# A two-layer, two-block transformer on one core: the scheduler's rule for choosing an engine, and new step orders for its four mixers

## The chip, the cores and the metric

The kernel runs on 1 core of a Trainium2 chip. The metric is the device time of one launch in microseconds (us), the median of several runs. Engines are named as in the profile: PE (matrix products), DVE (vector), ACT (scalar), POOL (GpSimd), SP (issues DMAs).

## What is computed

Sequence 512, width 1024, batch 1, fp32. Two blocks follow each other, each of two layers, and every layer is a mixer and a feed-forward network with residuals and RMS norms:

```python
# first block
h = h + nsa_mixer(rms_norm(h), ...)       # 16 heads: compressed, selected and window attention, gated
h = h + conv_ffn(rms_norm(h), ...)        # d_ff 2816, width-3 convolution, silu gate
h = h + swa_sink_mixer(rms_norm(h), ...)  # sliding window with sinks, its own k and v norm
h = h + conv_ffn(rms_norm(h), ...)
# second block
x = x + even_mixer(rmsnorm(x), ...)       # window attention beside a multi-scale pool
x = x + sq_relu_mlp(rmsnorm(x), ...)      # d_ff 4096, (relu u)^2
x = x + odd_mixer(rmsnorm(x), ...)        # dense attention beside a bidirectional recurrence
x = x + sq_relu_mlp(rmsnorm(x), ...)
return rmsnorm(x)
```

In the traces the stretches are, roughly: nsa to 390 us, conv_ffn to 780, swa to 900, conv_ffn to 1300, even to 1410, mlp to 1830, odd to 1990, mlp to the end.

## The kernel before

Activations lie transposed, as 128 x 512 tiles. Each fp32 operand of a large product is split in a high and a low half in a format that PE takes at full rate, and a product is three matmuls: high x high, high x low, low x high. `load` (L824) brings one unit of weights, 128 x 1024, by a 512 KB DMA into a `raw` buffer (4 of them), makes the high half with `copy` (L777) and the low half `raw - high` with `sub` (L803), both into one of 3 `W` buffers. `proj` (L841) is a load and 24 matmuls of 512 columns.

The program isn't emitted as it is written. A recorder notes every operation, and `Recorder.order` (L507) plays them through a model of five engines: it goes from event to event, and at each a free engine takes the first operation of its ready list that finds its buffers free. What it writes out is a fixed sequence for each engine. An operation may name other engines that could do it (`alt`). Before the change another engine takes one only where the work queued on the home engine reaches a bound for that pair of engines (`SPILL`, L352, tested at L617 to L620). Home engines: `copy` and `affine` ACT with DVE as the other, `tt` with `spare` (and so `sub`) DVE with POOL as the other, `norm` (L796, the softmax division) POOL with DVE, `ptt` (L800) POOL alone, `square` ACT with POOL.

In the mixers the recorded order of the steps (projections `Q`, `K`; scores `a`; products `p`; halves `L`, `U` of the output projection; and so on) is a string in `ORDERS` (L357), which `play` (L1054) walks through.

Functions the prediction speaks of: `norm_out` (L917) is the epilogue of a layer's last product: for each of 8 columns it adds to the residual, splits gain x residual (`split`: a copy and one multiply-subtract), and adds the square into the sum for the norm. `stats` (L1756) turns that sum into a factor per token: transposes, a reduce, a small multiply-add, a power on POOL, transposes, a copy. `tables` (L966) multiplies the two rotary tables by it. `rope` (L973) copies a projection from PSUM, has its halves swapped by DMA, and makes two products and an add. `qstack` (L991) splits the result into two stacked operands of 64 partitions each, two copies and two subtractions, and only then can the scores' matmuls of that query start.

Of the kernel before, what the change touches and what calls it, by code (L numbers as in the profile page):

```python
# [15 lines left out]
P = 128  # L16
# [321 lines left out]
def _width(v):  # L338
# [15 lines left out]
BOOST = 0  # L354
DMAQ = 2.0
HORIZON = 3000
ORDERS = {  # L357
# [33 lines left out]
class Recorder:  # L391
# [115 lines left out]
    def order(self):  # L507
# [31 lines left out]

        def oldest(kind):  # L540
            w = waiting[kind]
            while first[kind] < len(w) and w[first[kind]] in given:
                first[kind] += 1
            return w[first[kind]] if first[kind] < len(w) else -1
# [49 lines left out]
        while left:  # L594
# [7 lines left out]
            for e in engines:  # L602
# [7 lines left out]
                while i < min(len(ready[e]) - 1, 200):  # L610
# [6 lines left out]
                    if op.eng != e:  # L617
                        queue = sum(o.cost for _, _, o in ready[op.eng][:12] if not o.done)
                        if queue + max(0, free_at[op.eng] - now) < SPILL[op.eng, e]:
                            continue  # L620
                    if e == "scalar" and op.table and table not in op.table and now - op.ready < PATIENCE:
                        if now - switched < PATIENCE or any(not o.table or table in o.table for _, _, o in ready[e][i + 1:]):
                            heapq.heappush(events, max(switched, op.ready) + PATIENCE + 1e-6)
                            continue
# [88 lines left out]
def F(ap):  # L713
    return ap.bitcast(F32)


def _body(tc, ctx, d, out):
# [78 lines left out]
    def norm(o, i, a, b):  # L796
        nc.gpsimd.tensor_scalar(o, i, a, b, op0=OP.mult, op1=OP.mult, alt=[
            ["vector", "tensor_scalar", (o, i, a, b), {"op0": OP.mult, "op1": OP.mult}]])

    def ptt(o, a, b, op):  # L800
        nc.gpsimd.tensor_tensor(out=o, in0=a, in1=b, op=op)
# [171 lines left out]
    def rope(ps, cs, half):  # L973
# [11 lines left out]
        tt(o, sw, cs[1], OP.mult)  # L985
# [75 lines left out]
    def nsa(x, epi, prepare, half):  # L1061
# [189 lines left out]
        def scores(g, qb, ty, h0):  # L1251
# [21 lines left out]
            nc.vector.reciprocal(sm[:, 0:nh], sm[:, 0:nh])  # L1273
            for i, (r, t) in enumerate(who):
# [588 lines left out]
```

## Time and profile before

| | us |
|---|---|
| median of 3 runs (2398.35 to 2403.59) | 2403.03 |
| the profiled execution's own time | 2399.78 |
| its span, first to last instruction | 2397.9 |

| engine | busy us | share of the span |
|---|---|---|
| PE | 2280.3 | 95% |
| DVE | 1760.9 | 73% |
| POOL | 1254.6 | 52% |
| ACT | 701.8 | 29% |

PE's granted clock has a mean of 0.976 of full speed. The times of single instructions overlap a little on one engine, since one starts while the last one drains; the busy times here count such overlap once. The profile gives nearly every instruction the line of `emit` (L698), so tiles and shapes tell groups apart: `W<-raw` is the high half of a weight unit, `W<-raw,W` its low half, `S` a 128 x 512 working tile, `D` a double one, `bank` a PSUM bank, `par` per-channel constants, `small` per-token numbers.

### The profile page before, as it was taken

How to read it: one execution, taken by the hardware profiler on the slowest of the kernel's cores; microseconds unless marked ns; L12 is line 12 of the kernel's file. 1: busy time of each engine (PE TensorE's matmuls, PEld its weight loads, DVE VectorE, ACT ScalarE, POOL GpSimd, SP SyncE). 2: the span in 40 equal slices, each digit the busy share in tenths (PEclk: the TensorE clock that was granted, in tenths of full speed). 3: DMA queues.
4: the chain of work that ended last, by engine and by line, in shares of the span. 5: the costliest groups of instructions: out<-in, count | busy, mean ns of one | idle time of the engine just before them, and what ended most of it. 6: DMA issues, size and time to landing. Idle time of an engine off the chain costs nothing.

```text
span 2397.9 us, 28536 instructions
## 1 busy us (share of the span) xinstructions
PE 2280.3 (95%) x10565; PEld 1857.6 (77%) x10565; DVE 1760.9 (73%) x2429; ACT 701.8 (29%) x1353; POOL 1254.6 (52%) x865
## 2 busy tenths in 40 slices
PE   9878999999999799999999799999999789999998
PEld 7766678888888578888888578888887568888888
DVE  7978888949499999949499897345358899643546
ACT  4435653202023463202014342000014584100003
POOL 5755636444447855444437745444466565444445
PEclk9979999999999899999999899999999989999999
DMA  6421102232225212332225213332243201222224
GB/s 208 137 75 49 54 23 88 97 106 97 97 84 185 87 36 85 101 106 97 97 82 182 71 52 99 102 109 97 97 154 115 66 27 62 97 97 97 97 97 132
DMA packets 77243, 230.02 MB, mean 96 GB/s; under 512 B 10288, under 2 KB 12976, under 8 KB 77104
## 3 DMA queue, kind: packets, MB, share of 16 engines
q1 hardware_dynamic: 75584, 226.89, 29.1%
q8 instruction: 83, 1.36, 0.2%
q10 hardware_dynamic: 1520, 1.32, 0.2%
q14 instruction: 56, 0.46, 0.1%
HBM read 206.67 MB, written 8.39 MB: 90 GB/s over the span
## 4 chain that ended last, share of the span: by engine, by line
PE 56%; DVE 6%; ACT 2%; issue 1%; POOL 1%; SPq 0%; DMA 0%; DVEq 0%; ACTq 0%; POOLq 0%
PE bank L698 56%; DVE S L698 4%; DVE small L698 1%; ACT S L698 1%; DVE D L698 1%; POOL S L698 0%; DVE W L698 0%; ACT W L698 0%; ACT L698 0%; POOL W L698 0%; ACT D L698 0%; SPq L698 0%; DVE bank L698 0%; DMA S<-S 0%; DVEq L1850 0%
## 5 line engine op out<-in xcount | busy, mean ns | idle before, releaser
L698 PE MATMUL bank<-S,W 128*128 128x512 f32 (+1 forms) x7972 | 1809.3, 387 | 9.9 <-POOL W L698 5.9
L698 PEld LDWEIGHTS bank<-S,W 128*128 128x128 f32 x7972 | 1472.6, 189 | 313.3 <-DVE S L698 7.8
L698 POOL TENSOR_TENSOR W<-raw,W 128x1024 fp32r<-128x1024 f32 (+2 forms) x288 | 693.3, 2408 | 708.3 <-DVE W L698 541.8
L698 DVE CAST W<-raw 128x1024 fp32r<-128x1024 f32 (+2 forms) x246 | 179.8, 731 | 460.5 <-issue 319.3
L698 POOL TENSOR_TENSOR S<-S,S 128x512 f32<-128x512 f32 (+3 forms) x203 | 327.4, 1618 | 234.7 <-DVE S L698 157.7
L698 ACT ACTIVATE S<-S 128x512 f32<-128x512 f32 (+2 forms) x220 | 137.4, 627 | 969.6 <-DVE S L698 951.9
L698 DVE TENSOR_TENSOR S<-bank,S 128x512 f32<-128x512 f32 (+5 forms) x429 | 264.5, 632 | 14.5 <-ACT S L698 7.0
L698 DVE SCALAR_TENSOR_TENSOR S<-S,par,S 128x511 f32<-128x511 f32 (+3 forms) x236 | 250.2, 1069 | 7.7 <-ACT S L698 2.6
L698 ACT ACTIVATE W<-raw 128x1024 fp32r<-128x1024 f32 (+2 forms) x132 | 133.7, 1015 | 298.2 <-PE bank L698 242.8
L698 DVE TENSOR_TENSOR S<-S,S 128x512 fp32r<-128x512 f32 (+3 forms) x210 | 193.4, 926 | 16.8 <-ACT S L698 4.7
L698 PE MATMUL bank<-S,D 128*128 128x512 f32 (+3 forms) x387 | 138.4, 431 | 26.1 <-DVE S L698 13.5
L698 DVE CAST S<-S 128x512 fp32r<-128x512 f32 (+1 forms) x126 | 120.2, 954 | 48.7 <-ACT S L698 44.0
L698 ACT ACTIVATE S<-bank,small 128x256 f32<-128x256 f32 (+6 forms) x245 | 127.5, 530 | 83.3 <-DVE small L698 74.8
L698 ACT ACTIVATE S<-bank 128x512 fp32r<-128x512 f32 (+5 forms) x179 | 102.8, 588 | 137.9 <-PE bank L698 116.1
L698 PE MATMUL bank<-D,W 128*128 128x512 f32 x536 | 139.8, 397 | 0.6 <-DVE W L698 0.6
L698 DVE TENSOR_TENSOR W<-raw,W 128x1024 fp32r<-128x1024 f32 (+2 forms) x90 | 124.7, 1385 | 13.6 <-ACT W L698 13.0
L698 PE MATMUL bank<-cst,S 128*128 128x128 f32 x710 | 115.5, 283 | 13.6 <-DVE S L698 7.9
L698 DVE TENSOR_REDUCE small<-bank 128x1 f32<-128x512 f32 (+7 forms) x201 | 119.9, 614 | 6.8 <-PE bank L698 5.2
L698 PEld LDWEIGHTS bank<-D,W 128*128 128x128 f32 x536 | 99.1, 188 | 20.4 <-ACT S L698 0.8
L698 PEld LDWEIGHTS bank<-cst,S 128*128 128x128 f32 x710 | 88.0, 145 | 33.8 <-DVE S L698 8.3
L698 DVE TENSOR_SCALAR S<-S,par 128x512 f32<-128x512 f32 (+1 forms) x62 | 112.3, 1812 | 2.1
L698 PEld LDWEIGHTS bank<-S,D 128*128 128x128 f32 x387 | 70.4, 197 | 51.4 <-DVE S L698 24.9
(122 smaller groups left out, 1398.3 us busy)
## 6 DMA issues: line engine op xcount, KB each, us to landing
raw<-in_f_in_dram SPq DMA_DIRECT2D x88, 512.0 KB, 3.2
raw<-in_m_out_dram SPq DMA_DIRECT2D x72, 512.0 KB, 3.2
raw<-in_m_in_dram SPq DMA_DIRECT2D x64, 512.0 KB, 3.3
raw<-in_f_out_dram SPq DMA_DIRECT2D x32, 512.0 KB, 3.2
raw<-in_a_in_dram SPq DMA_DIRECT2D x17, 512.0 KB, 3.5
raw<-in_o_in_dram SPq DMA_DIRECT2D x15, 512.0 KB, 3.4
S<-S SPq DMA_DIRECT2D x116, 64.0 KB, 2.0
raw<-in_f_out_dram SPq DMA_DIRECT2D x16, 384.0 KB, 2.9
```

What stands on the lines that cost most here:

```text
L698: r = getattr(getattr(nc, op.eng), name)(*args, **kw)
```

## The change

Three things are changed.

First, the rule for the engine: for an operation with alternatives, a free engine takes it only if no other of its engines would, by the scheduler's own prices, end it sooner. An engine's end is its queue, plus the operation's latency, plus a tax of once its price on DVE and on POOL. `SPILL` is no longer used.

Second, more operations may move: `ptt` may go to DVE, `norm` also to ACT, the sine product of `rope` to POOL. For ACT to do it, `norm` now has one factor: where nsa multiplied by the reciprocal and by the gate, the gate is multiplied into the reciprocal first, in one small DVE operation for each `scores`.

Third, the four strings in `ORDERS` are new permutations of the same steps. A line each of the first string shows it; the test that keeps ACT's function table also leaves out operations too far ahead.

```diff
+TAX = {"gpsimd": 1.0, "vector": 1.0}
+MARGIN = {}
+DEEP = 12
...
-    "nsa": "S01 Q01 G S00 c00 K00 a0312 Q00 S11 S10 K01 a0222 a0310 Q11 a0213 c01 c02 a0112 a0010 c10 c11 "
+    "nsa": "G Q01 S01 S00 c00 K00 a0312 Q00 S11 S10 K01 a0222 a0310 Q11 c03 c01 c02 a0112 c11 a0010 c12 c10 "
...
+        def cost_on(op, e):
+            return (op.cost, op.lat, op.lock) if e == op.eng else op.alt[e][1]
+
+        def best(op, e):
+
+            def wait(x):
+                lock = cost_on(op, x)[2]
+                return max(0.0, held["P"] - now) if lock == "D" else max(0.0, held["D"] - now) if lock else 0.0
+            here = wait(e) + cost_on(op, e)[1] + TAX.get(e, 0.0) * cost_on(op, e)[0]
+            for x in (op.eng, *op.alt):
+                if x == e:
+                    continue
+                q = max(0.0, free_at[x] - now)
+                for _, _, o in ready[x][:DEEP]:
+                    if o is op:
+                        break
+                    if not o.done and o.eng == x:
+                        q += o.cost
+                there = max(q, wait(x)) + cost_on(op, x)[1] + TAX.get(x, 0.0) * cost_on(op, x)[0]
+                if there + MARGIN.get((x, e), 0.0) < here:
+                    return False
+            return True
...
-                    if op.eng != e:
-                        queue = sum(o.cost for _, _, o in ready[op.eng][:12] if not o.done)
-                        if queue + max(0, free_at[op.eng] - now) < SPILL[op.eng, e]:
-                            continue
+                    if op.alt and not best(op, e):
+                        continue
...
-                        if now - switched < PATIENCE or any(not o.table or table in o.table for _, _, o in ready[e][i + 1:]):
+                        if now - switched < PATIENCE or any(
+                                (not o.table or table in o.table) and o.n <= front + HORIZON
+                                for _, _, o in ready[e][i + 1:]):
...
-    def norm(o, i, a, b):
-        nc.gpsimd.tensor_scalar(o, i, a, b, op0=OP.mult, op1=OP.mult, alt=[
-            ["vector", "tensor_scalar", (o, i, a, b), {"op0": OP.mult, "op1": OP.mult}]])
+    def norm(o, i, a):
+        nc.gpsimd.tensor_scalar(o, i, a, None, op0=OP.mult, alt=[
+            ["vector", "tensor_scalar", (o, i, a, None), {"op0": OP.mult}],
+            ["scalar", "activation", (o, i, AF.Copy), {"scale": a}]])
 
     def ptt(o, a, b, op):
-        nc.gpsimd.tensor_tensor(out=o, in0=a, in1=b, op=op)
+        kw = dict(out=o, in0=a, in1=b, op=op)
+        nc.gpsimd.tensor_tensor(**kw, alt=[["vector", "tensor_tensor", (), kw]])
...
-        tt(o, sw, cs[1], OP.mult)
+        tt(o, sw, cs[1], OP.mult, True)
...
+            tt(sv, sv, gv, OP.mult)
             for i, (r, t) in enumerate(who):
                 ei = F(e)[:, i * wd:(i + 1) * wd]
-                gi = 3 * (4 * g + r) + t
-                norm(ei, ei, sm[:, i:i + 1], gates[:, qb, gi:gi + 1])
+                norm(ei, ei, sm[:, i:i + 1])
...
-                norm(ei, ei, sm[:, i:i + 1], 1.0)
+                norm(ei, ei, sm[:, i:i + 1])
```

Counted over the whole program, by the instructions of each engine in the two programs:

| | before | changed |
|---|---|---|
| POOL, all | 870 | 275 |
| low halves of weights on POOL (`W<-raw,W`) | 288 | 0 |
| low halves of weights on DVE | 90 | 378 |
| high halves of weights on DVE (`W<-raw`) | 246 | 10 |
| high halves of weights on ACT | 132 | 368 |
| DVE, all | 2428 | 2791 |
| ACT, all | 1106 | 1424 |
| PE, all (unchanged work) | 10732 | 10732 |

Two places show it. The first is DVE's sequence in the middle of the first conv_ffn, for one pair of input projections (up and gate): the multiplication by the token factor, `affine`, two taps of the convolution, the product of the pair, the split of the result. Before:

```order
L698 TENSOR_TENSOR S45_6023<-bank2_5981,S35_4151 128x512
L698 CAST S24_6027<-S22_5994 128x512
L698 TENSOR_TENSOR W2_6020<-raw1_5890,W2_6020 128x1024
L698 SCALAR_TENSOR_TENSOR S46_6030<-S45_6023,par_66,S46_6030 128x511
L698 SCALAR_TENSOR_TENSOR S46_6030<-S45_6023,par_66,S46_6030 128x510
L698 CAST W0_6061<-raw2_5927 128x1024
L698 TENSOR_TENSOR S10_6066<-bank3_6018,S35_4151 128x512
L698 TENSOR_SCALAR S15_6072<-S10_6066,par_66 128x512
L698 SCALAR_TENSOR_TENSOR S15_6072<-S10_6066,par_66,S15_6072 128x511
L698 SCALAR_TENSOR_TENSOR S15_6072<-S10_6066,par_66,S15_6072 128x510
L698 TENSOR_TENSOR S15_6072<-S46_6030,S15_6072 128x512
```

Changed:

```order
L723 TENSOR_TENSOR S48_6116<-bank4_6069,S47_4224 128x512
L723 TENSOR_SCALAR S29_6121<-S48_6116,par_66 128x512
L723 TENSOR_TENSOR W1_6112<-raw1_5976,W1_6112 128x1024
L723 SCALAR_TENSOR_TENSOR S29_6121<-S48_6116,par_66,S29_6121 128x511
L723 SCALAR_TENSOR_TENSOR S29_6121<-S48_6116,par_66,S29_6121 128x510
L723 TENSOR_TENSOR S23_6151<-bank3_6110,S47_4224 128x512
L723 TENSOR_SCALAR S12_6157<-S23_6151,par_66 128x512
L723 TENSOR_TENSOR W0_6149<-raw2_6013,W0_6149 128x1024
...
L723 TENSOR_TENSOR S12_6157<-S29_6121,S12_6157 128x512
L723 CAST S8_6182<-S12_6157 128x512
L723 TENSOR_TENSOR S28_6186<-S12_6157,S8_6182 128x512
```

Both low halves of a pair's weights and the low half of its result now stand on DVE; one of the weights' and the result's were POOL's. The cast of a weight unit has left DVE for ACT.

The second is DVE's sequence at the start of swa, from the reduce in `stats` over the tables and the first key or query's `rope` to its first 64-partition split. Before:

```order
L698 TENSOR_REDUCE small9_6686<-bank4_6670 128x4
L698 TENSOR_TENSOR W1_6675<-raw2_6549,W1_6675 128x1024
L698 TENSOR_SCALAR small9_6686<-small9_6686 128x4
L698 COPY S41_6729<-bank5_6722 128x512
L698 COPY S19_6738<-bank0_6679 128x512
L698 TENSOR_TENSOR W2_6733<-raw3_6585,W2_6733 128x1024
L698 TENSOR_TENSOR S11_6681<-S11_6681,S27_4833 128x512
L698 TENSOR_TENSOR S34_6701<-S34_6701,S27_4833 128x512
L698 TENSOR_TENSOR S11_6681<-S11_6681,S15_6766 128x512
L698 TENSOR_TENSOR S48_6745<-S48_6745,S27_4833 128x512
L698 TENSOR_TENSOR S33_6819<-S11_6681,S33_6819 64x512
```

Changed:

```order
L723 TENSOR_TENSOR W0_6731<-raw1_6587,W0_6731 128x1024
L723 TENSOR_REDUCE small10_6752<-bank0_6738 128x4
L723 TENSOR_SCALAR small10_6752<-small10_6752 128x4
L723 COPY S28_6776<-bank2_6770 128x512
L723 TENSOR_TENSOR S30_4914<-S30_4914,S28_6776 128x512
L723 TENSOR_TENSOR S24_4919<-S24_4919,S28_6776 128x512
L723 TENSOR_TENSOR W2_6784<-raw2_6631,W2_6784 128x1024
L723 TENSOR_TENSOR S3_6744<-S3_6744,S24_4919 128x512
L723 TENSOR_TENSOR S27_6816<-S23_6791,S30_4914 128x512
L723 TENSOR_TENSOR S3_6744<-S3_6744,S8_6794 128x512
...
L723 TENSOR_TENSOR S19_6826<-S3_6744,S19_6826 64x512
```

The weights' subtraction stands ahead of the reduce and no longer between it and the small multiply-add; the two products of the tables (`S30_4914` and `S24_4919`), which were POOL's, follow the copy on DVE. Between the last two rows shown stand a cast of the same split and a cast of weights.

## Rows read from the trace of the kernel before

**Rows 1.** The page: busy us, share and instructions by engine.

```profile
PE 2280.3 (95%) x10565; PEld 1857.6 (77%) x10565; DVE 1760.9 (73%) x2429; ACT 701.8 (29%) x1353; POOL 1254.6 (52%) x865
```

**Rows 2.** Stretches: start and end, length, busy us of each engine (instructions), PE's clock, DMA.

```profile
90.00:270.00 180.00, 143.99 (x718) 111.01 (x716) 151.36 (x264) 87.66 (x221) 110.13 (x111) 0.87 0.25 77
...
390.00:735.00 345.00, 345.00 (x1524) 284.32 (x1523) 261.95 (x295) 59.96 (x78) 151.95 (x70) 1.00 0.31 99
...
780.00:840.00 60.00, 44.58 (x198) 35.78 (x197) 56.61 (x90) 27.47 (x83) 49.81 (x55) 0.86 0.28 84
...
1320.00:1380.00 60.00, 42.20 (x183) 31.55 (x182) 53.14 (x119) 22.50 (x53) 47.83 (x42) 0.86 0.23 71
...
1830.00:1980.00 150.00, 119.39 (x488) 91.02 (x487) 131.56 (x175) 104.92 (x168) 91.50 (x71) 0.91 0.21 63
...
2370.00:2398.00 28.00, 17.95 (x147) 17.29 (x145) 14.16 (x22) 9.93 (x19) 16.77 (x15) 0.89 0.27 93
```

**Rows 3.** DVE by tiles: count, shortest/median/longest ns, first and last start, shapes.

```profile
L698 DVE TENSOR_TENSOR S<-bank,S x429: 399/681/693, 125.2 to 2381.4; 128x512 f32<-128x512 f32 x60, 128x512 fp32r<-128x512 f32 x55, 64x256 f32<-64x256 f32 x23, 64x512 fp32r<-64x512 f32 x4
...
L698 DVE SCALAR_TENSOR_TENSOR S<-S,par,S x236: 737/751/2889, 5.5 to 2034.2; 128x511 f32<-128x511 f32 x47, 128x510 f32<-128x510 f32 x46, 128x512 fp32r<-128x512 f32 x23, 128x512 f32<-128x512 f32 x2
L698 DVE TENSOR_TENSOR S<-S,S x210: 411/693/2884, 27.7 to 2394.2; 128x512 fp32r<-128x512 f32 x46, 128x512 f32<-128x512 f32 x43, 64x512 fp32r<-64x512 f32 x10, 128x256 f32<-128x256 f32 x6
...
L698 DVE CAST S<-S x126: 408/1380/2546, 49.2 to 2342.5; 128x512 fp32r<-128x512 f32 x114, 64x512 fp32r<-64x512 f32 x12
...
L698 DVE TENSOR_TENSOR W<-raw,W x90: 691/1225/2815, 4.8 to 2379.7; 128x1024 fp32r<-128x1024 f32 x77, 128x512 fp32r<-128x512 f32 x7, 128x768 fp32r<-128x768 f32 x5, 128x640 fp32r<-128x640 f32 x1
...
L698 DVE TENSOR_SCALAR S<-S,par x62: 475/2121/2756, 372.7 to 1815.5; 128x512 f32<-128x512 f32 x48, 128x512 fp32r<-128x512 f32 x14
```

**Rows 4.** POOL by tiles, the same columns.

```profile
L698 POOL TENSOR_TENSOR W<-raw,W x288: 1290/2392/2954, 13.6 to 2376.8; 128x1024 fp32r<-128x1024 f32 x136, 128x768 fp32r<-128x768 f32 x6, 128x512 fp32r<-128x512 f32 x2
L698 POOL TENSOR_TENSOR S<-S,S x203: 730/1618/2285, 7.9 to 2392.5; 128x512 f32<-128x512 f32 x57, 128x512 fp32r<-128x512 f32 x30, 128x256 f32<-128x256 f32 x9, 64x512 fp32r<-64x512 f32 x6
```

**Rows 5.** The page's groups for the weights' high halves: busy us, mean ns | idle before.

```profile
L698 DVE CAST W<-raw 128x1024 fp32r<-128x1024 f32 (+2 forms) x246 | 179.8, 731 | 460.5 <-issue 319.3
...
L698 ACT ACTIVATE W<-raw 128x1024 fp32r<-128x1024 f32 (+2 forms) x132 | 133.7, 1015 | 298.2 <-PE bank L698 242.8
```

**Rows 6.** Timeline, the start of swa: start us, us, instructions merged under one start.

```profile
751.49 5.90 DVE L698 SCALAR_TENSOR_TENSOR S<-S,par,S 128x512 fp32r<-128x512 f32 x4
...
761.68 0.68 DVE L698 TENSOR_REDUCE small<-bank 128x4 f32<-128x512 f32 x1
762.28 2.81 DVE L698 TENSOR_TENSOR W<-raw,W 128x1024 fp32r<-128x1024 f32 x1
...
765.02 0.16 DVE L698 TENSOR_SCALAR small<-small 128x4 f32<-128x4 f32 x1
...
767.89 6.48 POOL L698 TENSOR_TENSOR S<-S,S 128x512 f32<-128x512 f32 x4 [1.62 <-DVE S L698]
...
771.46 7.97 DVE L698 TENSOR_TENSOR S<-S,S 128x512 f32<-128x512 f32 x4 [1.18 <-DMA S<-S]
...
777.76 1.28 ACT L698 ACTIVATE S<-S 64x512 fp32r<-64x512 f32 x2 [3.35 <-DVE S L698]
```

**Rows 7.** Timeline around a stall of PE in even.

```profile
1342.35 1.95 DVE L698 TENSOR_SCALAR S<-S,small 128x384 f32<-128x384 f32 x2
...
1347.14 1.69 DVE L698 TENSOR_TENSOR S<-S,S 128x512 f32<-128x512 f32 x1
...
1348.36 3.27 POOL L698 TENSOR_TENSOR D<-S,D 64x512 fp32r<-64x512 f32 x2
...
1350.00 1.01 PE L698 MATMUL bank<-S,D 128*128 128x384 f32 x2 [9.93 <-POOL D L698]
```

**Rows 8.** Timeline around a stall of PE in odd.

```profile
1911.03 1.50 DVE L698 CAST S<-S 128x512 fp32r<-128x512 f32 x1
...
1919.25 0.80 PE L698 MATMUL bank<-S,S 128*128 128x512 f32 x1 [10.71 <-ACT S L698]
```

More of the change, by code (lines that the diff above doesn't have):

```diff
@@ L1273, in scores @@
             nc.vector.reciprocal(sm[:, 0:nh], sm[:, 0:nh])
+            gi = 3 * (4 * g + who[0][0]) + who[0][1]
+            if qb == 0:
+                gv = gates[:, qb, gi - 1:gi + 5].rearrange("p (r t) -> p r t", t=3)[:, :, 1:3]
+                sv = sm[:, 0:nh].rearrange("p (r t) -> p r t", t=2)
+            else:
+                gv, sv = gates[:, qb, gi:gi + 3 * nh - 2:3], sm[:, 0:nh]
+            tt(sv, sv, gv, OP.mult)
             for i, (r, t) in enumerate(who):
                 ei = F(e)[:, i * wd:(i + 1) * wd]
-                gi = 3 * (4 * g + r) + t
-                norm(ei, ei, sm[:, i:i + 1], gates[:, qb, gi:gi + 1])
+                norm(ei, ei, sm[:, i:i + 1])
                 heads[g, qb, t, r] = ei
@@ L1717, in scores @@
             nc.vector.reciprocal(sm[:, 0:1], sm[:, 0:1])
-            norm(F(e), F(e), sm[:, 0:1], 1.0)
+            norm(F(e), F(e), sm[:, 0:1])
             es[n, qb] = e
```

51 rows, old and new, of the table ORDERS are left out of this document.

## The prediction

> **What bounds the kernel now.** I read the page first. PE is busy for 2280.3 of 2397.9 us [rows 1], so 117.6 us is all the time in which it does nothing, and no faster engine elsewhere can pay more than that, but for the clock. Then the stretches. In the first conv_ffn PE is busy for the whole of 345.00 us at a clock of 1.00 [rows 2]: there PE alone decides, and whatever the change does on the other engines is worth nothing as long as it stays hidden. Four stretches are different, one at the start of each mixer. PE stands still for 180 - 144.0 = 36.0 us in nsa, 60 - 44.6 = 15.4 in swa, 60 - 42.2 = 17.8 in even and 150 - 119.4 = 30.6 in odd [rows 2]; together 99.8 of the 117.6. In these same four the granted clock falls to 0.87, 0.86, 0.86 and 0.91, from the higher of its two levels (2.4 GHz) to the lower (1.2 GHz) for a part of the time, while PE waits between its matmuls. A stretch of t us at clock c loses up to (1 - c) t: 23.4, 8.4, 8.4 and 13.5 us. What can be won is so at most 59, 24, 26 and 44 us, 153 in all, somewhat less since the low clock costs nothing while PE idles. The last 28 us (10 idle) and the start are not touched.
>
> Who is late there? In swa DVE is busy 56.6 of 60 us and in even 53.1 of 60, with POOL at 49.8 and 47.8 [rows 2]. The third view, DVE by tiles, shows why DVE is so full: the same operation takes very different times. Where one input comes from PSUM it takes 681 ns at the median and never over 693. With its inputs in SBUF alone the median is often the same 693, but the longest 2884; a cast that can take 408 has a median of 1380, and the scale-and-bias operation of `affine`, at best 475, one of 2121 [rows 3]. The long ones are about as long as a free one and one of POOL's operations of 1.6 to 2.4 us [rows 4] together, and operations on PSUM show none: I read this as two engines that hold each other up in SBUF. So POOL costs twice, by its own slowness (2392 ns for a weight subtraction that DVE does in 1225 at the median, 1.22 below) and by what it does to DVE.
>
> **The change, part by part.** *Weights.* All 288 subtractions leave POOL and 236 casts leave DVE for ACT. DVE gets 288 x 1.22 = 351 us and gives up 236 x 0.73 = 172 [rows 3, 5]; ACT gets 236 x 1.02 = 240 us, from a busy share of 29% [rows 1]. In conv_ffn this must stay under PE. A pair of input projections costs DVE, in the changed order, twice (0.68 + 0.55 + 1.22 + 0.75 + 0.75) for the PSUM product, `affine`, the weights and two taps, and 0.69 + 0.42 + 0.69 for the pair's product and split: 9.7 us. (0.55 for `affine` lies just over the shortest of its group, 0.475; at that group's present median of 2.12 the pair would be 12.8.) PE needs 48 matmuls x 345.00/1524 = 10.9 us [rows 2]. So DVE is hidden at 89% if POOL's absence takes the waiting away, and not hidden if it stays; POOL is left with 275 of 870 instructions and almost none of them in these stretches, so I take the former. Cost: 0, covered by PE. The latency of a unit, cast then subtraction, goes from 0.73 + 2.39 to 1.02 + 1.22, shorter, with three buffers in front of it.
>
> *Start of swa.* Four multiply-subtracts of the epilogue take 5.90 us [rows 6], free ones 4 x 0.75 = 3.0: 2.9 saved. The reduce ends at 762.36, but the small multiply-add starts at 765.02, behind a weights' subtraction of 2.81 us that itself waits for POOL. In the changed order that subtraction stands ahead of the reduce: 2.6 saved. The two tables are two of POOL's four products, 2 x 1.62 = 3.2 us, then 2 x 0.69 on DVE: 1.8 saved. `rope` goes from 771.46 to the copies at 777.76, 6.3 us; in the changed order there stand one weights' subtraction and three operations, 1.22 + 3 x 0.69 = 3.3: 3.0 saved. Together 10.3 us earlier for the first key or query. PE is fed by projections meanwhile, so this is worth something only if the later queries move along; DVE's queue is nearly gapless there, so I count **10** of the 24, with 0 and 24 as the ends.
>
> *Start of even.* The epilogue and `stats` are the same functions, and I count the same 10 for the lead. Inside the longest stall, 9.93 us, a DVE sum takes 1.69 for 0.69, two normalizations 1.95 where the shortest scale in SBUF is 0.48 each, and the subtraction that ends it is one of two on POOL in 3.27 us, 0.69 on DVE [rows 3, 7]: 1.0 + 1.0 + 0.9 = 2.9. The two overlap, so **12** of 26; ends 0 and 26.
>
> *nsa and odd.* Their chains have the same kinds in them; in odd's longest stall (10.71 us) a cast takes 1.50 for 0.41 [rows 3, 8], a tenth of the stall. But here DVE's sums speak against a large gain. POOL works 110.1 us in nsa's stretch; at 1.22/2.39 that is 56 on DVE, on top of 151.4 in a stretch of 180; in odd 91.5 becomes 47, on top of 131.6 of 150 [rows 2 to 4]. Both would overflow by 27 and 28 us if everything moved and no waiting vanished. A third of POOL's instructions stay, and the waiting does shrink, so I take a small gain of a sixth of nsa's 59 and a fifth of odd's 44: **10** and **9**; the ends are 0 or below (the slower case) and half, 30 and 22.
>
> *Small terms.* nsa gets 88 small multiplications on DVE. No row shows one, but the smallest operation in the rows is 0.16 us [rows 6]: 14 us beside other work, taken into the small share above; if they were all on the path, the 10 would be gone. Normalizations on ACT lie beside 87.7 us of its work in 180 [rows 2]. The new step orders themselves I price at nothing: they permute the same steps, from a gain like that of the stalls down to a loss like it.
>
> One rule of the Trainium skill speaks against the change. Its page Perfetto Trace Analysis, section Optimizing Scalar/DVE Operations, advises to move work from a saturated DVE to Scalar or even GPSIMD, and adds that moving between DVE and GPSIMD may not help since they share a read port. The change does the opposite in stretches where DVE is at 94%. By the first half of it the sum would be that of the slower case below; the second half is what rows 3 show, and no run here yet shows which of the two wins.
>
> **Sum.** 10 + 12 + 10 + 9 = 41 us off the profiled execution's own 2399.8 us, which is 2358.8. The median shown is 3.2 above that execution; the same put on top gives **2362**.
>
> **Rivals.** *The stalls dissolve.* If the waiting between the two engines is nearly all that makes the chains late, swa and even lose all 50 and nsa and odd half of 103: 101 us, 2302. For it: DVE is slowed fourfold in places [rows 3]. Against: chains with DMA hops and PSUM reads stay.
>
> *Swallowed.* Two thirds of POOL's work moves and no waiting goes in nsa and odd: 151 + 38 and 132 + 32 are 9 and 14 over, which takes back the 22 of swa and even: 2402. For it: DVE's sums; against: the free durations exist in hundreds.
>
> *DVE becomes the bound.* All POOL work of nsa and odd lands on a full DVE, and PE waits for its queue: 27 + 28 - 22 = 33 us more, 2436. It decides from the point where less than about half of the overflow of 55 is paid by waiting that vanishes. The rule above says this too.
>
> That the change doesn't do what it says is not a case: the instruction sequences show the moves.
>
> **How the numbers follow.** The forecast has 0.58, with its own range of 2330 to 2390; the dissolved stalls 0.14, the swallowed gain 0.15, the full DVE 0.13. A measurement of this kernel tells some 0.2%, 5 us, from no change: 2398 to 2408 is the same. Faster: 0.58 + 0.14 + 0.04 of the swallowed case = 0.76; same 0.07, its middle; slower 0.13 + 0.04 = 0.17. The range from 2305 to 2404 leaves out the full DVE and half of the dissolved stalls, 0.20, and reaches the ends of the four terms but for the deepest.
>
> **What would show it.** Right: POOL under 300 us busy, DVE's SBUF operations at medians near their shortest times, PE still gapless in conv_ffn, first scores of swa and even some 10 us earlier, their stretches with less than 10 us idle, and the clock in them above 0.90. Wrong: DVE busy for over 95% in the start of nsa or odd with PE's idle time there grown; or PE gaps inside conv_ffn that end with DVE, which would mean that the weights' subtractions come late; or stalls of the same length that end with ACT.

## The result and the profile after

The changed kernel takes 2333.55 us, the median of 4 runs (2331.64 to 2333.8), against 2403.31 before (one run more than in the table above): a ratio of 0.9713, 95% interval 0.9696 to 0.973. That is some 70 us less, where 41 were forecast; the time lies 28 below the forecast and inside its range. The profiled execution took 2331.64 us, its span is 2329.5.

The page's first part answers to [rows 1]:

```profile
PE 2257.8 (97%) x10561; PEld 1844.4 (79%) x10565; DVE 1719.9 (74%) x2792; ACT 968.8 (42%) x1671; POOL 242.0 (10%) x270
```

The span fell by 68.4 us. PE's idle time went from 117.6 to 2329.5 - 2257.8 = 71.7 us, which is 45.9; the other 22.5 are PE's own busy time for the same matmuls. I put them down to the clock: its mean rose from 0.976 to 0.988, so what it costs by the prediction's (1 - c) t falls from at most 57.5 us to at most 28.0. POOL went down to a fifth. DVE has 363 instructions more and is busy 41 us less.

The stretches, with the columns of [rows 2], moved along with the layers (swa's 28 us earlier, even's 42, odd's 59):

```profile
90.00:270.00 180.00, 156.76 (x821) 119.35 (x826) 169.46 (x408) 128.91 (x316) 38.76 (x33) 0.95 0.26 76
390.00:735.00 345.00, 345.00 (x1525) 285.33 (x1524) 253.96 (x349) 89.12 (x101) 0.76 (x1) 1.00 0.34 108
752.00:812.00 60.00, 55.09 (x292) 44.12 (x290) 57.91 (x130) 46.35 (x132) 18.81 (x33) 0.97 0.37 106
1278.00:1338.00 60.00, 54.95 (x268) 43.28 (x267) 58.58 (x151) 37.43 (x90) 20.02 (x18) 0.94 0.22 70
1771.00:1921.00 150.00, 128.15 (x537) 97.39 (x536) 142.36 (x226) 110.87 (x184) 21.97 (x18) 0.93 0.23 71
```

PE's idle time is 23.2, 4.9, 5.1 and 21.9 us in the four starts, where it was 36.0, 15.4, 17.8 and 30.6, and the clock stands at 0.93 to 0.97 where it was 0.86 to 0.91. conv_ffn is as gapless as before, with the weights' subtractions on DVE and POOL at rest.

DVE by tiles, with the columns of [rows 3]:

```profile
L723 DVE TENSOR_TENSOR S<-bank,S x412: 395/684/694, 103.2 to 1946.3; 128x512 f32<-128x512 f32 x61, 128x512 fp32r<-128x512 f32 x44, 64x256 f32<-64x256 f32 x27, 64x512 fp32r<-64x512 f32 x3
L723 DVE TENSOR_TENSOR S<-S,S x383: 411/685/1791, 8.2 to 2325.4; 128x512 f32<-128x512 f32 x90, 128x512 fp32r<-128x512 f32 x70, 64x512 fp32r<-64x512 f32 x21, 128x256 f32<-128x256 f32 x11
L723 DVE TENSOR_TENSOR W<-raw,W x378: 681/1225/2319, 4.4 to 2310.8; 128x1024 fp32r<-128x1024 f32 x174, 128x768 fp32r<-128x768 f32 x8, 128x512 fp32r<-128x512 f32 x7
...
L723 DVE TENSOR_SCALAR S<-S,par x105: 478/546/553, 349.6 to 1756.6; 128x512 f32<-128x512 f32 x84, 128x512 fp32r<-128x512 f32 x21
...
L723 DVE CAST S<-S x70: 404/427/429, 56.3 to 1976.7; 128x512 fp32r<-128x512 f32 x53, 64x512 fp32r<-64x512 f32 x17
```

The cast's median fell from 1380 to 427 ns and that of `affine` from 2121 to 546, and their longest lie a few ns above. What reads PSUM takes what it took. So what made casts and `affine` long in [rows 3] was waiting. It isn't gone everywhere: operations with two inputs in SBUF still take up to 1791 ns (2884 before), and the weights' subtractions up to 2319 (2815 before).

What PE waits for (us in total, times, longest):

```profile
PE bank L723 <- ACT S L723: 27.0, 23, 5.3
PE bank L723 <- DVE S L723: 20.2, 22, 3.2
PE bank L723 <- DVE W L723: 6.5, 7, 2.0
```

No stall of the size of those in [rows 7, 8] (9.93 and 10.71 us) is left, and POOL ends next to none.

**Where the time went, by layer.** I cut each trace at the reduce in `stats`, took each layer's length, and corrected it for the matmuls that slid over a cut (0.226 us each, from 345.00/1524 in [rows 2]; in nsa 18 fewer fall before its cut). Each row rests on the one profiled execution of its kernel. So done, the layers differ from the kernel before, in us, by:

| run | median | nsa | swa | even | odd | four feed-forwards |
|---|---|---|---|---|---|---|
| the change | 2333.6 | -22.9 | -16.0 | -17.2 | -9.7 | -1.8 |
| rule_old_orders | 2367.2 | -4.5 | -9.4 | -16.5 | 0.0 | -1.6 |
| new_orders_old_rule | 2372.6 | -14.9 | -2.5 | -7.1 | -1.0 | -0.2 |
| pool_reads | 2504.3 | +19.2 | +1.7 | -2.7 | +6.0 | +74.5 |
| pool_writes | 2367.4 | -2.4 | -8.2 | -14.8 | -6.0 | -1.1 |
| weights_alone | 2369.3 | -3.8 | -9.9 | -8.1 | -7.5 | -1.6 |
| weights_back | 2409.3 | +0.7 | +3.3 | +1.4 | +5.0 | 0.0 |
| products_on_pool | 2357.0 | -7.3 | -9.0 | -16.0 | -6.9 | -1.7 |
| tax_three | 2350.1 | -6.0 | -13.4 | -15.6 | -9.8 | -2.2 |
| one_swap | 2341.1 | -17.0 | -16.0 | -18.1 | -4.4 | -1.9 |
| nsa_old | 2354.4 | -4.1 | -16.2 | -18.5 | -4.0 | -2.0 |
| weights_new_orders | 2369.2 | -6.1 | -6.2 | -15.0 | -1.3 | -1.2 |
| norm_on_two | 2372.5 | -2.1 | -6.4 | -14.2 | -1.1 | -2.0 |

The feed-forward layers are PE's alone in all runs but one. Everything is decided in the four mixers.

### The profile page after: what moved, and what is told of

It is laid out like the page before. It is cut to its first block, busy times and chain, and to the rows that moved or that the text cites. A ratio compares the mean times of both kernels' runs of the same rounds, so it can differ in the third digit from the quotient of the medians.

```text
span 2329.5 us, 28430 instructions
## 1 busy us (share of the span) xinstructions
PE 2257.8 (97%) x10561; PEld 1844.4 (79%) x10565; DVE 1719.9 (74%) x2792; ACT 968.8 (42%) x1671; POOL 242.0 (10%) x270
## 3 DMA queue, kind: packets, MB, share of 16 engines
q1 hardware_dynamic: 75584, 226.89, 30.4%
## 4 chain that ended last, share of the span: by engine, by line
PE 80%; DVE 12%; ACT 4%; issue 2%; DMA 1%; SPq 1%; POOL 0%; DVEq 0%; ACTq 0%; POOLq 0%
PE bank L723 80%; DVE S L723 7%; ACT S L723 3%; DVE small L723 2%; DVE W L723 2%; DVE D L723 1%; DMA S<-S 1%; SPq L723 1%; ACT W L723 0%; ACT D L723 0%; POOL S L723 0%; DMA D<-D 0%; ACT L723 0%; DMA raw<-in_a_in_dram 0%; DVE bank L723 0%
## 5 line engine op out<-in xcount | busy, mean ns | idle before, releaser
L723 ACT ACTIVATE W<-raw 128x1024 fp32r<-128x1024 f32 (+2 forms) x368 | 381.3, 1037 | 949.2 <-PE bank L723 843.7
L723 DVE TENSOR_TENSOR W<-raw,W 128x1024 fp32r<-128x1024 f32 (+2 forms) x378 | 501.8, 1328 | 78.2 <-ACT W L723 76.7
L723 DVE TENSOR_TENSOR S<-S,S 128x512 f32<-128x512 f32 (+3 forms) x383 | 267.6, 707 | 14.1 <-ACT S L723 5.3
L723 ACT ACTIVATE S<-S 128x512 fp32r<-128x512 f32 (+2 forms) x219 | 137.0, 629 | 229.4 <-DVE S L723 167.6
L723 DVE SCALAR_TENSOR_TENSOR S<-S,par,S 128x511 f32<-128x511 f32 (+3 forms) x235 | 176.8, 757 | 3.5
L723 PE MATMUL bank<-S,D 128*128 128x512 f32 (+2 forms) x349 | 132.0, 433 | 15.8 <-ACT S L723 7.6
L723 ACT ACTIVATE S<-bank,small 128x512 f32<-128x512 f32 (+6 forms) x247 | 129.1, 531 | 35.7 <-DVE small L723 33.8
L723 ACT ACTIVATE S<-bank 128x512 fp32r<-128x512 f32 (+4 forms) x190 | 109.4, 591 | 53.8 <-PE bank L723 47.8
L723 DVE TENSOR_REDUCE small<-bank 128x1 f32<-128x512 f32 (+8 forms) x201 | 120.8, 614 | 8.5 <-PE bank L723 8.0
L723 POOL TENSOR_TENSOR small<-small,small 128x4 f32<-128x4 f32 (+1 forms) x13 | 13.4, 1031 | 986.5 <-DVE small L723 986.5
L723 PE MATMUL bank<-S,S 128*128 128x512 f32 (+3 forms) x280 | 73.9, 374 | 14.7 <-ACT S L723 10.8
```

Of the source, the lines that this page charges most:

```text
L723: r = getattr(getattr(nc, op.eng), name)(*args, **kw)
```

## The experiments

### The rule and the orders apart

`rule_old_orders` is the changed kernel with the four old strings; `new_orders_old_rule` the kernel before with the four new ones. One line of the first, against the changed kernel:

```diff
-    "nsa": "G Q01 S01 S00 c00 K00 a0312 Q00 S11 S10 K01 a0222 a0310 Q11 c03 c01 c02 a0112 c11 a0010 c12 c10 "
+    "nsa": "S01 Q01 G S00 c00 K00 a0312 Q00 S11 S10 K01 a0222 a0310 Q11 a0213 c01 c02 a0112 a0010 c10 c11 "
...
```

> The changed kernel with the four step orders of the kernel before: the new rule for the engine, the wider alternatives and the one-factor normalization stay. If the gain of 70 us comes from work leaving POOL (theory A), most of it stays: 2340 to 2365 us, POOL under 300 us busy, DVE's casts in SBUF at a median near 0.42 us. If it comes from the permuted steps (theory B): 2385 to 2405 us.

> The kernel before with the new step orders alone; the old rule, alternatives and normalization. Theory A: 2385 to 2410 us, POOL still over 1200 us busy. Theory B: 2335 to 2365 us. The new orders were made for other engine choices, so a loss against the kernel before is possible under A.

Measured: 2367.18 (ratio 0.9856, 0.9841 to 0.9871) and 2372.58 (0.9879, 0.9864 to 0.9893), 34.5 and 29.1 us below 2401.7, the kernel before as measured beside them (beside the later runs it took 2401.6 and 2403.6). Neither lies inside the range of either theory; the first is 2 us above A's. The two sum to 63.6 of some 70. The rule alone is worth about what I forecast for the whole change; the orders, which I priced at nothing, are worth nearly as much again. By the table the strings add, on top of the rule, 18.4 us in nsa, 9.7 in odd, 6.6 in swa and 0.7 in even.

### What POOL does to DVE by reading

Both kernels are the changed one with idle work on POOL, on a tile of its own that nothing else uses, behind every DVE operation that writes a `W` buffer (388 of them, 378 low and 10 high halves). One reads two inputs, the other only writes, for about the same time. To make room, the small buffers were halved and an unused tile was left out; every engine's own sequence stayed that of the changed kernel.

```diff
                 r = getattr(getattr(nc, op.eng), name)(*args, **kw)
+                if op.eng == "vector" and op.outs[0].buf.kind == "W":
+                    for _ in range(2):                                                     # pool_reads
+                        nc.gpsimd.tensor_tensor(out=idle, in0=idle, in1=idle, op=OP.mult)
+                    for _ in range(5):                                                     # pool_writes
+                        nc.gpsimd.memset(idle, 0.0)
```

> The changed kernel, and after each of DVE's 378 weight subtractions POOL gets two products of 128x448 on a tile that nothing else uses, about 2.2 us of reading and writing SBUF; DVE's, ACT's and PE's sequences are unchanged, and of POOL's own 270 operations each may queue behind one such pair. If two engines holding each other up in SBUF is the larger cost of POOL's work (A1), DVE's SBUF operations stretch as before the change and the time goes back to 2375 to 2400 us. If the cost was that POOL's own slow operations stood in the chains (A2), the time stays at 2333 to 2345.

> As the run before with five fills of the same tile (128x448, about 2.2 us, writes and no reads) in place of each pair of products. It occupies POOL as long, so what POOL's own operations lose in the queue is the same. If DVE is held up by POOL's reads (A1), this run stays at 2333 to 2345 us and DVE's durations stay short; if the queue on POOL is what costs, it is as slow as the run with the products.

Measured: 2504.34 (1.0423, 1.0408 to 1.0439) and 2367.36 (0.986, 0.9844 to 0.9877). The groups of POOL's idle work (count, busy us, mean ns, then idle time before it), first the reading kernel, then the writing one:

```profile
L726 POOL TENSOR_TENSOR pw<-pw 128x448 f32<-128x448 f32 x776 | 998.1, 1286 | 51.0
```

```profile
L726 POOL MEMSET pw<- 128x448 f32 x1940 | 939.7, 484 | 104.1
```

About the same occupation of POOL costs 137 us more when it reads. The writing itself costs 34 us against the changed kernel, all in the mixers, where POOL's own work now stands behind it. Both times lie above what either theory gave: reading is dearer than I thought, and a queue on POOL has a price of its own. In part it shows in what PE waits for; this line is the largest, and all waits that end with POOL sum to 13.9 us, where the changed kernel has 1.9:

```profile
PE bank L723 <- POOL small L723: 9.7, 2, 8.2
```

DVE's groups in the reading kernel:

```profile
L723 DVE TENSOR_TENSOR S<-S,S 128x512 f32<-128x512 f32 (+3 forms) x383 | 371.0, 977 | 19.0 <-ACT S L723 8.2 <-POOL S L723 3.6 <-DMA S<-S 2.5
L723 DVE SCALAR_TENSOR_TENSOR S<-S,par,S 128x511 f32<-128x511 f32 (+3 forms) x235 | 229.0, 978 | 3.4
...
L723 DVE CAST S<-S 128x512 fp32r<-128x512 f32 (+1 forms) x70 | 41.5, 593 | 3.0 <-ACT S L723 0.7 <-DMA S<-S 0.2
```

and the same in the writing kernel:

```profile
L723 DVE TENSOR_TENSOR S<-S,S 128x512 f32<-128x512 f32 (+3 forms) x383 | 266.3, 704 | 24.2 <-ACT S L723 8.2 <-POOL S L723 8.0 <-DMA S<-S 3.2
L723 DVE SCALAR_TENSOR_TENSOR S<-S,par,S 128x511 f32<-128x511 f32 (+3 forms) x235 | 175.1, 750 | 3.8 <-ACT S L723 0.2
...
L723 DVE CAST S<-S 128x512 fp32r<-128x512 f32 (+1 forms) x70 | 33.8, 483 | 6.8 <-DMA S<-S 4.1 <-ACT S L723 0.7
```

With no idle work these means are 707, 757 and 424 ns. Operations with two inputs in SBUF grow by 38% and 29% beside reads and not at all beside writes; casts grow beside both. The Trainium skill says the same of who holds up whom in its page SBUF — State Buffer, section Who interferes with whom: a DVE instruction with two SBUF inputs contends with a GpSimd instruction that reads SBUF, not with one that only writes, and a cast may contend with either. The runs agree with it.

Half of the 137 us is in conv_ffn, whose stretch in the reading kernel is no longer gapless:

```profile
400.00:745.00 345.00, 317.77 (x1351) 257.62 (x1350) 268.76 (x300) 75.91 (x84) 170.30 (x138) 0.96 0.26 88
```

So the prediction's cover (9.7 of 10.9 us of DVE per pair, hidden only if the waiting goes) was as thin as it looked: where POOL reads, DVE's pair outgrows PE's (from 477.8 to 493.0 us DVE is busy for 14.5 of the 15.2 us that a pair then takes, and PE's clock stands at 0.88), and some 35 us go in each conv_ffn.

### Which part of the rule pays

`weights_alone` is the kernel before with the weights' subtraction tied to DVE; `weights_back` the new rule with the old strings, and that subtraction tied to POOL; `products_on_pool` the changed kernel without the choice for `ptt`; `tax_three` the changed kernel with POOL's price three times as heavy in the tax; `norm_on_two` the changed kernel without ACT for `norm`.

```diff
-            sub(lo[:, c], raw[:, c], F(hi[:, c]))
+            tt(lo[:, c], raw[:, c], F(hi[:, c]), OP.subtract)                              # weights_alone
+            ptt0(lo[:, c], raw[:, c], F(hi[:, c]), OP.subtract)                            # weights_back
...
+    def ptt0(o, a, b, op):                                                                 # weights_back
+        nc.gpsimd.tensor_tensor(out=o, in0=a, in1=b, op=op)
...
-        nc.gpsimd.tensor_tensor(**kw, alt=[["vector", "tensor_tensor", (), kw]])
+        nc.gpsimd.tensor_tensor(**kw)                                                      # products_on_pool
...
-TAX = {"gpsimd": 1.0, "vector": 1.0}
+TAX = {"gpsimd": 3.0, "vector": 1.0}                                                       # tax_three
...
-            ["vector", "tensor_scalar", (o, i, a, None), {"op0": OP.mult}],                # norm_on_two
-            ["scalar", "activation", (o, i, AF.Copy), {"scale": a}]])
+            ["vector", "tensor_scalar", (o, i, a, None), {"op0": OP.mult}]])
```

> The kernel before (old rule, old orders) with one edit: the low halves of the weights are always subtracted on DVE; 288 instructions of 2.39 us leave POOL, and DVE gets 288 of about 1.22 us. Theory W (of the new rule's gain of 35 us, alone measured at 2367 against 2402, most is these 288 reads that leave SBUF to DVE): 2402 - 25 = 2377 or less, with PE still gapless in conv_ffn. Rival R (what pays are the products and normalizations of the chains that leave POOL, and the weights, which run ahead of PE, only load DVE): within 5 us of 2402 or above it. If DVE's queue is what matters, the casts that the old rule leaves on DVE show as PE gaps in conv_ffn, some 10 to 30 us above 2402.

> The new rule with the old orders (measured at 2367), with the low halves of all the weights forced back on POOL: 378 instructions of 2.4 us, some 900 us of POOL's time, reading SBUF beside DVE. Theory W: the gain of the rule goes, 2367 + 25 to 35 = 2392 to 2402, and the longest times of DVE's operations in SBUF come back. With reading as dear as in the run of POOL products (998 us of them cost 137 us more than the same time of writing), 900 us would cost up to 120 less what DVE is relieved of (378 x 1.33 = 500 us), so over 2402 is possible. Rival R: 2367 to 2375.

> The changed kernel (2333.6), with the operations that only POOL could do before (rotary products, products of the token factor with the tables and the like) tied to POOL again; about 100 instructions of 1.6 us, 165 us in all, go back. Theory W: they are few and lie in the chains of the mixers only, 2334 + 5 to 10 = 2339 to 2344. Rival R: they are the links of the chains that feed PE at the start of each mixer, 1 us slower each and waited for: 2334 + 15 to 25 = 2349 to 2359.

> The changed kernel (2333.6) with the tax on POOL's price 3 instead of 1: POOL keeps about 100 instructions of 270, DVE gets 92 more and ACT 59. If what POOL reads costs others as in the run of POOL products (0.14 us per us of POOL's time), the some 150 us of POOL's time that go are worth 20 us: 2314. If DVE at 97% in the starts of the mixers is the bound now, 92 x 0.6 = 55 us more of it, a good half of that in the mixers, cost 10 to 30 us: 2344 to 2364. Both may cancel: 2329 to 2339 would say that the tax of 1 is near the balance.

> The changed kernel (2333.6), in which the softmax divisions may not go to ACT: of its 136 some 104 go to DVE, 104 x 0.48 = 50 us more of DVE, and few to POOL. Theory R (DVE's queue in the mixers is what PE waits for, and any relief of it by ACT counts): half of the 50 us or more on the path, 2334 + 10 to 25 = 2344 to 2359. As I priced it in the prediction (free on ACT, and so no more than beside other work): 2334 to 2339.

Measured, in this order: 2369.34 (0.9869, 0.9852 to 0.9885), 2409.26 (1.0033, 1.0022 to 1.0044), 2357.03 (0.9814, 0.98 to 0.9829), 2350.11 (0.9785, 0.9771 to 0.98) and 2372.48 (0.9871, 0.9857 to 0.9886).

With the old strings the weights are all of the rule's gain: moving them alone gains 32 us, putting all 378 on POOL, 90 more than the kernel before has there, loses 42, and all else in the rule gains nothing on top of the weights (2369 and 2367). The page's first part of `weights_alone`:

```profile
PE 2267.4 (96%) x10561; PEld 1849.6 (78%) x10565; DVE 1759.2 (74%) x2642; ACT 752.7 (32%) x1430; POOL 551.6 (23%) x578
```

DVE took over 288 subtractions, 351 us at 1.22 each, gave up 57 casts in SBUF and a few `affine`, and is busy for as long as before, 1759 against 1761 us. On DVE, the waiting that went paid for the move. The reverse shows in `weights_back`: without the 378 subtractions, which last some 498 us together in `rule_old_orders`, DVE is busy for only 43.5 us less (1689.5 against 1733.0), because what is left takes longer; this group's mean is 751 ns in `rule_old_orders`:

```profile
L724 DVE SCALAR_TENSOR_TENSOR S<-S,par,S 128x511 f32<-128x511 f32 (+3 forms) x236 | 340.9, 1450 | 32.2 <-ACT S L724 28.2
```

That isn't yet PE's gain. The move also shortens POOL's queue, which costs by itself, as `pool_writes` shows. Of PE's idle time `weights_alone` takes away 19 us (117.6 before, 98.6 in it), and PE's waits that end with POOL fall by 16.5 of them, from 33.6 to 17.1 us; the other 13 us are PE's busy time. How the 32 us divide between DVE's waiting and POOL's queue no run separates.

The other three start from the changed kernel, and each costs time. The products cost 23.5 us on POOL, as theory R had it. The heavier tax takes POOL down to 43.7 us, and DVE's busy time too (1699.9), and yet costs 16.5 us, in the range that I gave for a full DVE: the price of 1000 us of reading doesn't scale down to the last 200. The divisions, which I had free on ACT, cost 38.9 us without it, more than any theory gave. The 109 more of them on DVE last 69.2 - 27.9 = 41 us together, so nearly every us of them would have to be waited for. In all three nsa falls back to what it had with the old string, which the next runs explain in part.

### Whose are the orders' 30 us?

`one_swap` exchanges two neighbours in nsa's new string, `nsa_old` has the old string for nsa alone, `weights_new_orders` is `weights_alone` with the four new strings.

```diff
-           "p0111 p0120 p0121 a0321 p0220 a1120 a1310 p0221 p0320 a1311 p0321 a1211 p0222 p0322 p0323 e00 e01 "
+           "p0111 p0120 p0121 a0321 p0220 a1120 a1310 p0221 a1311 p0320 p0321 a1211 p0222 p0322 p0323 e00 e01 "
```

> The changed kernel (2333.6) with two neighbours of nsa's new string, the product p0320 and the score a1311, back in their old sequence. No work is added or taken, DVE gets 6 instructions more, ACT 5 fewer, POOL 5 more, but from there to the end of odd the played sequence of all engines is another one (some 1600 rows of DVE's list differ). Theory F (fit: the strings' gain belongs to the one sequence that was searched out, and any other with the same steps is worth that of the old strings): most of the 18 us of nsa go, 2344 to 2352. Theory M (the gain is in which steps stand early and late, as the halves of the output projection): within 5 us of 2334.

> The changed kernel (2333.6) with the old string for nsa alone; the other three are new. By the stretches of the earlier runs, new against old strings are worth 18.4 us in nsa, 6.8 in swa, 0.9 in even and 10.0 in odd under the new rule. Theory M and additive parts: 2334 + 18 = 2352. If swa, even and odd were fitted to what nsa leaves (buffers, the queue ahead), they lose too: 2360 to 2367, the time with all four old strings. Under 2340 the stretches would have misled and the gain sits elsewhere.

> The kernel before (old rule) with two edits: low halves of the weights always on DVE, and the four new strings. Apart they took 32 us (2369) and 29 us (2373) off 2402. Theory M, additive: 2402 - 61 = 2341. Theory F: the strings were searched with the new rule, and here the sequences are again others; if the sum doesn't hold, 2355 to 2369. Under 2334 it would beat the change itself, and the rest of the rule would cost time.

Measured: 2341.10 (0.9741, 0.9724 to 0.9757), 2354.36 (0.9798, 0.9783 to 0.9812) and 2369.17 (0.9858, 0.9843 to 0.9873). The old string in nsa costs 20.8 us, 18.8 of them in nsa itself: nearly additive, as expected. But on the kernel with the weights moved and the old rule the new strings gain nothing at all (2369.17 against 2369.34), while with the weights on POOL they gained 29 and with the new rule 34. And the swap of two neighbours, which moves no work, costs 7.5 us, between what the two theories gave. By the profiled executions it is 10.1 us, 5.9 in nsa and 5.3 in odd, and in `nsa_old` odd loses 5.7 too: a string has changed in nsa, and a layer far behind it with its own string untouched moves with it. The swap's stretch at the start of nsa, and behind it that of `rule_old_orders`:

```profile
90.00:270.00 180.00, 157.88 (x816) 119.89 (x819) 164.80 (x398) 126.54 (x303) 39.81 (x33) 0.92 0.26 76
```

```profile
90.00:270.00 180.00, 151.36 (x732) 114.39 (x734) 158.90 (x367) 110.40 (x257) 30.95 (x31) 0.87 0.26 77
```

With the swap PE is busy for a little longer than in the changed kernel (157.88 us against 156.76) and does no more, at 0.92 instead of 0.95: that difference is the clock's. With the old string PE gets 84 matmuls fewer done in these 180 us than with the swap: it stands still for 6.5 us more, and the clock is at 0.87. So a string's value isn't its own. The new ones pay 0 to 34 us, by the rule that they are played with, and in nsa the whole 23 us is there only for the one pair of rule and string; the old rule has 15 of it. Of the runs that played this string with the new rule or a variant of it, the swap keeps 17 us, while `products_on_pool`, `tax_three`, `norm_on_two` and `pool_writes`, the last with its sequence unchanged and only its times shifted, keep 2 to 7.

What stays open is how much of the 23.5 us of the products and the 38.9 of the divisions is their own price and how much is the fit that they break. With the old strings the two together gain next to nothing, but either alone with the old strings was not tried.

## Why the prediction came out

**The cover of the weights: right.** Cost 0 in conv_ffn: from 442.1 to 453.0 us, one pair, DVE is busy for 9.5 of 10.9 us, where 9.7 were forecast. All four feed-forwards together moved by 1.8 us. `pool_reads` shows the other end: with POOL reading for as long there as before (170 us of the stretch, 151.95 in [rows 2]) the two conv_ffn take 70 us more.

**Waiting between DVE and POOL: right as to DVE**, shown by the reading and the writing kernel and by DVE's busy time in `weights_alone` and `weights_back`. That this waiting is what PE's 32 us come from is shown only in part: the prediction named two costs of POOL, its slowness and what it does to DVE, and the first, as a queue, has a share that stays open. The rival of a full DVE fell: DVE is busy for 94% of nsa's stretch and 95% of odd's, as it said, 18 and 11 us more than before [rows 2], but PE's idle time there shrank. The page Perfetto Trace Analysis of the Trainium skill, section Optimizing Scalar/DVE Operations, says that with a saturated DVE it may make sense to offload work to Scalar or even GPSIMD, and that a move between DVE and GPSIMD might not help. Here the opposite move, from GpSimd to DVE, gained 32 us, so the second half of it held, and GpSimd was the wrong place. For Scalar the first half held: without ACT for the divisions the changed kernel takes 38.9 us more, their fit included.

**The four terms.** By `rule_old_orders` swa's 10 measured 9.4, even's 12 measured 16.5, nsa's 10 measured 4.5 and odd's 9 measured 0.0: 41 forecast, 30.4 measured in the mixers. The doubt about DVE's sums in nsa and odd was right, and even the sixth and the fifth that I kept were too much; even was undervalued. So the sum came near the rule's own 34.5 us by luck in part, 14.5 us too much in nsa and odd against 4.5 too little in even; and the whole 70 us stayed inside the range because the range was wide. The result lies about midway between the forecast of 2362 and the 2302 of the rival in which the stalls dissolve.

**The step that failed** is "The new step orders themselves I price at nothing: they permute the same steps". They measured 29 us with the old rule and 34 with the new, 18.4 in nsa. The sizes fit into the 59 and 44 us that I had set as what can be won in nsa and odd; I had given a share of these to the rule and, between a gain and a loss of like size, none to the strings.

**What was to show it.** POOL under 300 us, DVE's medians near their shortest, under 10 us idle in swa and even, the clock above 0.90: all came. In swa DVE's parts came as counted: from reduce to small multiply-add 0.72 us where [rows 6] has 3.34, the two tables 1.29 us on DVE instead of 3.24 on POOL, and from the reduce to the first split's copies 8.8 us instead of 16.1:

```profile
733.27 0.68 DVE L723 TENSOR_REDUCE small<-bank 128x4 f32<-128x512 f32 x1
733.99 0.17 DVE L723 TENSOR_SCALAR small<-small 128x4 f32<-128x4 f32 x1
...
736.72 1.29 DVE L723 TENSOR_TENSOR S<-S,S 128x512 f32<-128x512 f32 x2
...
742.09 0.42 DVE L723 CAST S<-S 64x512 fp32r<-64x512 f32 x1
```

But the first scores didn't come 10 us earlier. PE's timeline after the change:

```profile
735.33 0.62 PE L723 MATMUL bank<-cst,small 128*128 128x128 f32 x4
735.71 22.49 PE L723 MATMUL bank<-S,W 128*128 128x512 f32 x98
758.22 0.33 PE L723 MATMUL bank<-S,S 128*128 128x128 f32 x1
...
772.93 0.44 PE L723 MATMUL bank<-S,S 128*128 128x128 f32 x2 [1.08 <-DVE S L723]
```

From the transposes of `stats` to the first score it takes 22.9 us, where it took 16.2. The new string puts more projections first (98 matmuls ahead of a score, 69 before), and then scores and projections alternate with no gap of over 1 us until 772.93. But the string isn't the reason: with the old one, in `rule_old_orders`, it takes 16.8 us, behind 72 projections, and swa gains 9.4 us all the same. In even the same distance went from 29.5 to 22.9, and to 23.1 with the old string. The gain is the gaps behind, not the lead: a step of mine that had the right size for a reason only half right.

## What to carry to other kernels

Look at the shortest and the longest beside the median of an operation before you call its engine full: what is waiting in it goes away with the neighbour that causes it, and the engine can then take over work and be no busier, as DVE did here with 288 subtractions. An order of steps has no price of its own: these four were worth 0 to 34 us by the rule and the placement that they were played with, so don't price one without the other, and don't take it for free because it only permutes. A single ablation of a kernel whose order fits its rule measures the fit that it breaks along with the part it removes, so cross it with another order before you give the part that price.

## What the runs showed of the hardware

POOL's reads and POOL's writes are different things for DVE: 998 us of products cost 137 us more than 940 us of memsets, in the same places of the same sequence. And PE's clock turns small gaps into larger losses: where `pool_reads` opens gaps in conv_ffn the clock falls from 1.00 to 0.96, and of the 68.4 us of span that the change takes away 22.5 are the same matmuls, done in less time at a higher mean clock, half as much again on top of the 45.9 of idle time that went.
